# RWKV-7 chunk scan: solution and next chunk's values by turns, last chunk's output behind them; the heads of the A products and the halves of the merge by turns

## The chip, the cores and the metric

The kernel runs on one NeuronCore of one Trainium2 chip. A core has a matrix engine (PE, with its weight loads listed as PEld), a vector engine (DVE), a scalar engine (ACT), a general engine (POOL) and a queue engine (SP), each with its own in-order instruction stream, and 16 DMA engines. The metric is the device time in microseconds; lower is better. [...]

## The reference

One decoder block, sequence 2048, width 1024, float32. One projection of the normed input feeds two token mixers; their outputs are projected, gated, merged, projected again and added to the residual stream. The change lies in the second mixer, a delta-rule recurrence with 16 heads of width 64:

```
def step(state, inp):
    r_t, w_t, k_t, v_t, kk_t, b_t = inp
    sk = jnp.einsum('bhvk,bhk->bhv', state, kk_t)
    state = (state * w_t[:, :, None, :] - sk[..., None] * b_t[:, :, None, :]
             + v_t[..., None] * k_t[:, :, None, :])
    return state, jnp.einsum('bhvk,bhk->bhv', state, r_t)
```

## The kernel before

The sequence is cut into 4 blocks of 512 tokens (`b`), the heads into 4 groups of 4 (`g`), so there are 16 calls of `group`. A group holds two pairs of heads (`q`), a pair two heads (`hh`), and a block 8 chunks of 64 tokens (`c`, with `e = c % 2`). Inside a chunk the recurrence is solved in closed form:

- `pair` prepares one pair of heads. It projects keys, receptances and values (`shifted`, whose products are recorded at L195 in the helper `mm3k`), forms `KR` and `BK`, and multiplies them into the score matrices ("A products", L525), which DVE masks into `As` (L527). The stationary operand there is `BKz`, a copy of `BK` in which the other head's 64 rows are zero, so that each product uses all 128 rows. ACT makes that copy (L518).
- `group` then inverts the triangular 64x64 blocks in `As`: the 32x32 diagonal blocks on POOL (L594 and L596), and the off-diagonal 32x32 blocks by two rounds of products ("the merge", L626 and L635), first all of `e = 0`, then all of `e = 1`, in one PSUM bank `pq`.
- The chunk scan runs over the 8 chunks. PE multiplies the state into `xo` (L668) and adds the part that comes from the chunk's own values `uv` (L673). DVE copies that to `X` (L676). PE multiplies `X` by the inverse (the solution, L682), DVE scales it into `uv` (L684), PE forms the state's update (L688), and DVE applies it (L693). The chunk's output `o` (`olast`, L653) is formed one chunk later and copied by ACT (L655).

A PE product uses as many rows of the array as its operands have partitions, and as many columns as its output has. A product on fewer than 128 rows or columns stands on a tile of the array; which one follows from the start partitions of operands (rows) and output (columns). `prow(e)` and `vrow(e)` name the two halves of the partitions, swapped between even and odd chunks. In before the scan uses 64x64 tiles (L673, L682), 128x64 tiles (L653) and the whole array (L668, L688); the profile writes this as `64*64`, `128*64`, `128*128`. A float32 product is two PE instructions (hence L525 x1024 for 512 products). The projections are float32r, one instruction each.

The order on each engine is made by a list scheduler from the program order and priorities before the kernel runs. While a scan waits, it puts projections (L195) of the gates and the convolution in between. Scan, A products and merge of one group therefore lie among the projections and preparation of others.

Of the kernel before, what the change touches and what calls it, by code (L numbers as in the profile page):

```python
# [2 lines left out]

# [6 lines left out]
F32 = mybir.dt.float32  # L10
# [3 lines left out]
ALU = mybir.AluOpType  # L14
# [4 lines left out]
P = 128  # L19
# [4 lines left out]
CH = 64  # L24
NCH = TB // CH
# [57 lines left out]
def hybrid_block(ctx: ExitStack, tc: tile.TileContext, x, vecs, convk, w2a2, final_g, ada, w_in, w_co, w_ro, w_o, crow, out,  # L83
                 seq=2048, groups=(0, 1, 2, 3), phase2=True, dbg=None):
    nc = tc.nc
# [46 lines left out]
    def flat(ap):  # L132
        return ap.rearrange("p a b -> p (a b)")
# [114 lines left out]
    pa = late.enter_context(tc.tile_pool(name="pa", bufs=PAB, space=PSUM))  # L248
# [23 lines left out]
    def headsum(ps, full, hi):  # L272
# [4 lines left out]
    BKz = c1.tile([P, 2, NCH // 2, 4 * CH], F32, name="BKz")  # L277
    nc.gpsimd.memset(BKz[64:128, 0], 0.0)
    nc.gpsimd.memset(BKz[0:64, 1], 0.0)
    hones = bones.bitcast(F32)[:, 0::64]  # L280
    one = c1.tile([P, CH], F32, name="one")
    nc.vector.memset(one, 1.0)
    maskA = c1.tile([P, 4, CH], F32, name="maskA")
# [154 lines left out]
    def prow(e):  # L438
        return slice(64, 128) if e == 0 else slice(0, 64)

    def vrow(e):
        return slice(0, 64) if e == 0 else slice(64, 128)

    kcol, rcol = prow, vrow

    def pair(b, q_, pr, h, lora, uv, Asb, rn, res):
# [12 lines left out]
        pq = pa.tile([P, TB], F32, name="aux", tag="aux")  # L459
# [12 lines left out]
        pe = l3.tile([P, NCH], F32, name="pe", tag="pe", bufs=4)  # L472
# [3 lines left out]
        KR = l3.tile([P, NCH // 2, 4 * CH], F32, name="KR", tag="KR", bufs=KRB)  # L476
        BK = l3.tile([P, NCH // 2, 4 * CH], F32, name="BK", tag="BK", bufs=BKB)
# [14 lines left out]
        for c in range(NCH):  # L492
            nc.tensor.matmul(pss[prow(c % 2), c // 2, :], sq[:, c * CH:c * CH + CH], hones, start=True, stop=True,
                             skip_group_check=True)
# [6 lines left out]
                                       scalar=hkk[:, pr:pr + 1], in1=E2.rearrange("p (c n) -> p c n", n=2 * CH),  # L501
                                       op0=ALU.mult, op1=ALU.mult)
# [13 lines left out]
        for hh in range(2):  # L516
            hs = slice(64 * hh, 64 * hh + 64)
            nc.scalar.copy(BKz[hs, hh], BK[hs])  # L518
        for c4 in range(NCH // 4):
            for hh in range(2):  # L520
                pA = pa.tile([P, 2, 256], F32, name="aux", tag="aux")
                for c in range(4):
                    cc, e = (c4 * 4 + c) // 2, c % 2
                    es = slice(e * 128, e * 128 + 128)
                    nc.tensor.matmul(pA[:, c // 2, es], BKz[:, hh, cc, es], KR[:, cc, es],  # L525
                                     start=(c == 0), stop=(c == 3), skip_group_check=True)
                nc.vector.tensor_tensor(  # L527
                    out=Asb[:, hh, c4 * 4:c4 * 4 + 4, :].rearrange("p (a e) n -> p a (e n)", e=2),
                    in0=pA, in1=flat(maskA).unsqueeze(1).broadcast_to([P, 2, 256]), op=ALU.mult)
        for e in range(2):  # L530
            sl = prow(e)
            tri = Asb[sl, :, e::2, kcol(e)]
# [18 lines left out]
        tk = l3.tile([P, NCH, P], F32, name="tk", tag="tk", bufs=TKB)  # L551
# [8 lines left out]

    def group(b, g, h, lora, fill):
        uv = l3.tile([P, NCH, 2, P], F32, name="uv", tag="uv", bufs=2)
        As = [l3.tile([P, 2, NCH, P], F32, name="As", tag="As", bufs=ASB) for _ in range(2)]
        R = [{}, {}]
        rn = lt.tile([P, 2, NCH // 2, 2], F32, name="rn", tag="rn")
# [51 lines left out]
        pq = pl.tile([P, 2, 2, NCH // 2, 32], F32, name="late", tag="late")  # L617
        for e in range(2):
            lo_, hi_ = quarters(e)
            for q in range(2):  # L620
                for hh in range(2):
                    nc.vector.transpose(T11[lo_, q, hh], As[q][lo_, hh, e::2, lo_])
        for e in range(2):
            lo_, hi_ = quarters(e)
            for n, (q, hh, c) in enumerate(every):
                nc.tensor.matmul(pq[hi_, q, hh, c, :], As[q][lo_, hh, 2 * c + e, hi_], T11[lo_, q, hh, c, :],  # L626
                                 start=(n == 0), stop=(n == 15), skip_group_check=True)
        for e in range(2):
            lo_, hi_ = quarters(e)
            nc.vector.tensor_copy(Qs[hi_], pq[hi_])  # L630

        for e in range(2):
            lo_, hi_ = quarters(e)
            for n, (q, hh, c) in enumerate(every):
                nc.tensor.matmul(pq[lo_, q, hh, c, :], Qs[hi_, q, hh, c, :], As[q][hi_, hh, 2 * c + e, hi_],  # L635
                                 start=(n == 0), stop=(n == 15), skip_group_check=True)
        for e in range(2):
            lo_, hi_ = quarters(e)
            for q in range(2):
                nc.vector.tensor_copy(As[q][lo_, :, e::2, hi_], pq[lo_, q])  # L640


        O = uv[:, 0::2]
        Sg = S[g]
        prev = None

        def olast(c, xo):

            vr, rc = vrow(c % 2), rcol(c % 2)
            for q in range(2):  # L650
                for hh in range(2):
                    hs = slice(64 * hh, 64 * hh + 64)
                    nc.tensor.matmul(xo[vr, q, hs], As[q][:, hh, c, rc], uv[:, c, q, hs],  # L653
                                     start=False, stop=(q == 1 and hh == 1), skip_group_check=True)
            nc.scalar.copy(O[vr, c // 2], xo[vr, 0:2])  # L655

        for c in range(NCH):
            cc, e = c // 2, c % 2
            pr_, vr = prow(e), vrow(e)
# [6 lines left out]
            xo = px.tile([P, 4, P], F32, name="xo", tag="xo")  # L666
            for q in range(2):
                nc.tensor.matmul(xo[:, q, :], R[q]["KR"][:, cc, es], Sg[:, q, :], start=(q == 0), stop=False,  # L668
                                 skip_group_check=True)
            for q in range(2):  # L670
                for hh in range(2):
                    hs = slice(64 * hh, 64 * hh + 64)
                    nc.tensor.matmul(xo[pr_, q, hs], As[q][vr, hh, c, kcol(e)], uv[vr, c, q, hs],  # L673
                                     start=False, stop=False, skip_group_check=True)
            X = lt.tile([P, 2, P], F32, name="X", tag="X", bufs=1)
            nc.vector.tensor_copy(X[pr_], xo[pr_, 0:2])  # L676
            if prev:
                olast(*prev)
            for q in range(2):
                for hh in range(2):  # L680
                    hs = slice(64 * hh, 64 * hh + 64)
                    nc.tensor.matmul(xo[pr_, q, hs], As[q][pr_, hh, c, kcol(e)], X[pr_, q, hs],  # L682
                                     start=(q == 0 and hh == 0), stop=(q == 1 and hh == 1), skip_group_check=True)
            nc.vector.tensor_tensor(out=uv[pr_, c].rearrange("p q (h n) -> p q h n", n=64),  # L684
                                    in0=xo[pr_, 0:2].rearrange("p q (h n) -> p q h n", n=64),
                                    in1=rn[pr_, :, cc, :].unsqueeze(3).broadcast_to([64, 2, 2, 64]), op=ALU.mult)
            for q in range(2):
                nc.tensor.matmul(xo[:, 2 + q, :], R[q]["tk"][:, c, :], uv[:, c, q, :], start=False, stop=(q == 1),  # L688
                                 skip_group_check=True)
            for q in range(2):  # L690
                for hh in range(2):
                    hs = slice(64 * hh, 64 * hh + 64)
                    nc.vector.scalar_tensor_tensor(out=Sg[hs, q, hs], in0=xo[hs, 2 + q, hs],  # L693
                                                   scalar=R[q]["pe"][hs, c:c + 1], in1=Se[hs, q, hs],
                                                   op0=ALU.mult, op1=ALU.add)
            prev = (c, xo)
        olast(*prev)


        O16 = O.rearrange("p a q (h n) -> p a (q h) n", n=64)  # L700
# [426 lines left out]
```

## Time and profile before

| | before |
|---|---|
| median of 3 runs | 3123.53 us (3115.43 to 3130.16) |
| profiled execution | 3119.74 us |
| its span | 3118.0 us |
| PE busy | 2980.5 us (96%) |
| DVE busy | 2138.2 us (69%) |
| POOL busy | 1142.4 us (37%) |
| ACT busy | 1018.6 us (33%) |
| mean granted TensorE clock | 0.984 |

Busy time on PE counts an instruction from its start to a modelled end, and instructions overlap there, so the rate at which PE works is read from the distance between starts, in the timeline of instructions. In that view a row is a run of like instructions of a line: start, time to the end of the last, number. The 16 groups lie between about 90 and 2640 us of the span; behind them come the output projections.

### The profile page before, as it was taken

What the parts mean: (1) busy time and instruction counts of PE and PEld (TensorE: products, weight loads), DVE (VectorE), ACT (ScalarE), POOL (GpSimd) and SP (SyncE); (2) the same over time, 40 slices, a digit from 0 to 9 for tenths busy, and PEclk for the clock granted to TensorE, in tenths of its full rate; (3) what the DMA queues carried; (4) which work ended last, traced back from release to release, by engine and by line L of the source; (5) the groups of instructions that cost most, each with busy time, mean ns of one, the idle gap of its engine ahead of it and who ended that gap; (6) DMA issues with size and microseconds to landing.
All of it is one profiled execution on the core that took longest, in us unless ns stands there. A gap on an engine that the chain in (4) does not pass through costs nothing. (4 is left out here: it accounts for less than half of the span.)

```text
span 3118.0 us, 64926 instructions
## 1 busy us (share of the span) xinstructions
PE 2980.5 (96%) x25648; PEld 2804.4 (90%) x25648; DVE 2138.2 (69%) x4282; ACT 1018.6 (33%) x1868; POOL 1142.4 (37%) x1708
## 2 busy tenths in 40 slices
PE   6799998999999999999999999999999999799998
PEld 6689998989999999999999999999999978678888
DVE  6676867686767676767676677767688535986633
ACT  4424343433233332323232414132332213342311
POOL 3354435433433325142424335316256013653100
PEclk9899999999999999999999999999999999899999
DMA  7665758573747476547565767646458657777665
GB/s 297 214 239 193 258 187 278 192 236 133 251 139 256 136 242 230 197 138 233 159 221 166 260 211 262 196 142 208 139 178 267 215 204 271 282 250 274 216 223 176
DMA packets 354849, 667.79 MB, mean 214 GB/s; under 512 B 134704, under 2 KB 153456, under 8 KB 354544
## 3 DMA queue, kind: packets, MB, share of 16 engines
q1 hardware_dynamic: 354544, 663.64, 63.2%
q8 instruction: 202, 3.31, 0.4%
q14 instruction: 103, 0.84, 0.1%
HBM read 483.07 MB, written 179.31 MB: 212 GB/s over the span
## 5 line engine op out<-in xcount | busy, mean ns | idle before, releaser
L195 PE MATMUL ps_main<-h_hi,w_hi 128*128 128x256 f32 x4608 | 958.1, 285 | 24.4 <-ACT w_hi L178 19.1
L195 PE MATMUL ps_main<-h_hi,w_lo 128*128 128x256 f32 x4608 | 958.6, 285 | 9.0 <-POOL w_lo L180 7.6
L195 PE MATMUL ps_main<-h_lo,w_hi 128*128 128x256 f32 x4608 | 958.1, 285 | 0.0
L195 PEld LDWEIGHTS ps_main<-h_hi,w_hi 128*128 128x128 f32 x4608 | 718.3, 189 | 35.9 <-ACT w_hi L178 20.2
L195 PEld LDWEIGHTS ps_main<-h_hi,w_lo 128*128 128x128 f32 x4608 | 716.7, 189 | 18.0 <-POOL w_lo L180 9.4
L195 PEld LDWEIGHTS ps_main<-h_lo,w_hi 128*128 128x128 f32 x4608 | 716.3, 189 | 7.3 <-issue 0.7
L759 DVE SCALAR_TENSOR_TENSOR acc<-u,ck,acc 128x512 f32<-128x512 f32 x928 | 698.0, 752 | 20.1
L594 POOL TENSOR_TENSOR itmp<-La,TT 128x126 f32<-128x126 f32 (+22 forms) x496 | 179.4, 362 | 147.5 <-DMA La<-dA 112.0
L693 DVE SCALAR_TENSOR_TENSOR S<-xo,pe,Se 64x64 f32<-64x64 f32 x512 | 144.9, 283 | 107.9 <-PE xo L688 98.6
L178 ACT CAST w_hi<-w_st 128x1024 fp32r<-128x1024 f32 x103 | 107.9, 1048 | 293.7 <-DMA w_st<-w_in_t 144.0
L596 POOL TENSOR_TENSOR TT<-TT,itmp 128x126 f32<-128x126 f32 (+22 forms) x496 | 190.0, 383 | 35.8
L663 ACT ACTIVATE Se<-S,pe 128x128 f32<-128x128 f32 x256 | 88.9, 394 | 228.7 <-DVE S L693 228.3
L180 POOL TENSOR_TENSOR w_lo<-w_st,w_hi 128x1024 fp32r<-128x1024 f32 x47 | 112.2, 2388 | 136.8 <-ACT w_hi L178 98.2
L548 POOL TENSOR_TENSOR vv<-rk,vv 128x512 f32<-128x512 f32 x32 | 43.5, 1359 | 295.7 <-ACT rk L547 295.7
L684 DVE TENSOR_TENSOR uv<-xo,rn 64x256 f32<-64x256 f32 x128 | 53.8, 421 | 131.8 <-PE xo L682 130.7
L525 PE MATMUL aux<-KR,BKz 128*128 128x128 f32 x1024 | 136.6, 278 | 2.6 <-DVE As L527 1.8
L180 DVE TENSOR_TENSOR w_lo<-w_st,w_hi 128x1024 fp32r<-128x1024 f32 x56 | 75.6, 1349 | 82.4 <-PE ps_main L195 51.3
L525 PEld LDWEIGHTS aux<-KR,BKz 128*128 128x128 f32 x1024 | 123.8, 191 | 5.0 <-DVE As L527 2.0
L527 DVE TENSOR_TENSOR As<-aux,maskA 128x512 f32<-128x512 f32 x128 | 86.9, 687 | 46.7 <-PE aux L525 46.1
L676 DVE COPY X<-xo 64x256 f32<-64x256 f32 x128 | 53.7, 420 | 91.6 <-PE xo L673 90.7
L655 ACT COPY uv<-xo 64x256 f32<-64x256 f32 x128 | 46.8, 366 | 186.2 <-PE xo L653 185.7
L668 PE MATMUL xo<-S,KR 128*128 128x128 f32 x512 | 95.7, 279 | 1.2 <-DVE S L693 1.1
(290 smaller groups left out, 5497.5 us busy)
## 6 DMA issues: line engine op xcount, KB each, us to landing
w_hi<-kh_in SPq DMA_DIRECT2D x219, 512.0 KB, 3.9
w_lo<-kl_in SPq DMA_DIRECT2D x219, 512.0 KB, 5.0
w_st<-w_in_t SPq DMA_DIRECT2D x73, 512.0 KB, 4.6
kh_in<-w_hi SPq DMA_DIRECT2D x71, 512.0 KB, 3.0
kl_in<-w_lo SPq DMA_DIRECT2D x71, 512.0 KB, 4.5
w_hi<-kh_ro SPq DMA_DIRECT2D x32, 512.0 KB, 4.3
w_lo<-kl_ro SPq DMA_DIRECT2D x32, 512.0 KB, 5.8
w_st<-w_co_t SPq DMA_DIRECT2D x32, 512.0 KB, 3.5
```

The costliest lines, as they stand in the source:

```text
L178: nc.scalar.copy(hi, st)
L180: lo_eng.tensor_tensor(out=lo, in0=st, in1=hi.bitcast(F32), op=ALU.subtract)
L195: nc.tensor.matmul(ps[:, qs], ww[:, k, :], aa[k][:, qs], start=(k == 0 and t == 0 and q == 0), stop=(k == KT - 1 and t == 2 and q == ms - ...
L525: nc.tensor.matmul(pA[:, c // 2, es], BKz[:, hh, cc, es], KR[:, cc, es], start=(c == 0), stop=(c == 3), skip_group_check=True)
L527: nc.vector.tensor_tensor(out=Asb[:, hh, c4 * 4:c4 * 4 + 4, :].rearrange("p (a e) n -> p a (e n)", e=2), in0=pA, in1=flat(maskA).unsqueeze ...
L594: nc.gpsimd.tensor_tensor(out=tmp[:, :ni, :nt], in0=La[:, j:j + 1, j + 1:].broadcast_to([P, ni, nt]), in1=TT[:, :ni, j:j + 1].broadcast_to ...
L596: nc.gpsimd.tensor_tensor(out=TT[:, :ni, j + 1:], in0=TT[:, :ni, j + 1:], in1=tmp[:, :ni, :nt], op=ALU.add)
L663: nc.scalar.mul(Se[:, q, :], Sg[:, q, :], R[q]["pe"][:, c:c + 1])
L668: nc.tensor.matmul(xo[:, q, :], R[q]["KR"][:, cc, es], Sg[:, q, :], start=(q == 0), stop=False, skip_group_check=True)
L684: nc.vector.tensor_tensor(out=uv[pr_, c].rearrange("p q (h n) -> p q h n", n=64), in0=xo[pr_, 0:2].rearrange("p q (h n) -> p q h n", n=64) ...
L693: nc.vector.scalar_tensor_tensor(out=Sg[hs, q, hs], in0=xo[hs, 2 + q, hs], scalar=R[q]["pe"][hs, c:c + 1], in1=Se[hs, q, hs], op0=ALU.mult ...
L759: nc.vector.scalar_tensor_tensor(out=acc if i + 1 < HALO else yj, in0=u[:, i:i + TB], scalar=ck[:, j, i:i + 1], in1=acc, op0=ALU.mult, op1 ...
```

## The change

Three places are changed.

**A products.** `BKz` and its copies go. Each head's product takes its own 64 rows of `BK` and `KR` (a 64x128 tile), and the program writes the two heads by turns, into two PSUM buffers `pA[0]` and `pA[1]` that are both taken before the first product.

**Merge.** The two halves `e` get a PSUM bank each (`pq[1]` from the pool `aux`, which `pair` uses as well), and the products of the halves are written by turns, in a fixed order (`issue_after` keeps an instruction behind another on its engine).

**Scan.** The solution and the values' part are products on 128 rows: `Xz` and `uv` hold zeros in the other 64 rows (POOL clears `uv` at each group's start, L563, and `Xz` once). The values' part of chunk `c + 1` (`xval`) is written by turns with the solution of chunk `c`, and `olast(c - 1)` follows directly; ACT copies the values' part to `Xz` (`xcopy`), and DVE adds the state's part to it in place of the copy to `X`. The two PSUM tiles `xo` belong to even and odd chunks throughout a group.

```
         for c4 in range(NCH // 4):
+            pA = [pa.tile([P, 2, 256], F32, name="aux", tag="aux") for _ in range(2)]
...
+                for hh in range(2):
+                    hs = slice(64 * hh, 64 * hh + 64)
+                    nc.tensor.matmul(pA[hh][:, c // 2, es], BK[hs, cc, es], KR[hs, cc, es],
+                                     start=(c == 0), stop=(c == 3), skip_group_check=True)
             for hh in range(2):
-                pA = pa.tile([P, 2, 256], F32, name="aux", tag="aux")
...
-                    nc.tensor.matmul(pA[:, c // 2, es], BKz[:, hh, cc, es], KR[:, cc, es],
...
+        for e in range(2):
+            nc.gpsimd.memset(uv[prow(e), e::2], 0.0)
...
+        pq = [p_.tile([P, 2, 2, NCH // 2, 32], F32, name=n_, tag=n_) for p_, n_ in ((pl, "late"), (pa, "aux"))]
...
+            for n, (q, hh, c) in enumerate(every[::-1]):
+                for e in range(2):
+                    with tc.issue_after(mm[-1].ins) if mm else nullcontext():
+                        mm_ = mul(e, q, hh, c, dict(start=(n == 0), stop=(n == 15), skip_group_check=True))
+                    mm = mm if n else mm + [mm_]
...
+        xo = [px.tile([P, 4, P], F32, name="xo", tag="xo") for _ in range(2)]
...
+            nc.tensor.matmul(xo[c % 2][prow(c % 2), 2 + q, hs], As[q][:, hh, c, kcol(c % 2)], uv[:, c, q, hs],
+                             start=(n == 0), stop=(n == 3), skip_group_check=True)
...
+            nc.scalar.copy(Xz[prow(c % 2), c % 2], xo[c % 2][prow(c % 2), 2:4])
...
-                    nc.tensor.matmul(xo[pr_, q, hs], As[q][vr, hh, c, kcol(e)], uv[vr, c, q, hs],
...
-            nc.vector.tensor_copy(X[pr_], xo[pr_, 0:2])
-            if prev:
-                olast(*prev)
...
-                    nc.tensor.matmul(xo[pr_, q, hs], As[q][pr_, hh, c, kcol(e)], X[pr_, q, hs],
...
+            nc.vector.tensor_tensor(out=Xz[pr_, e], in0=b_[pr_, 0:2], in1=Xz[pr_, e], op=ALU.add)
...
+            for n, (q, hh, hs) in enumerate(every):
+                with tc.issue_after(mm.ins) if n else nullcontext():
+                    mm_ = nc.tensor.matmul(b_[pr_, q, hs], As[q][:, hh, c, kcol(e)], Xz[:, e, q, hs],
+                                           start=(n == 0), stop=(n == 3), skip_group_check=True)
+                mm = mm if n else mm_
+                if c + 1 < NCH:
+                    with tc.issue_after(mm.ins):
+                        xval(c + 1, n)
+            if c:
+                with tc.issue_after(mm.ins):
+                    olast(c - 1)
+            if c + 1 < NCH:
+                xcopy(c + 1)
+            if c:
+                ocopy(c - 1)
```

Lines of the changed kernel that the prediction names: A products L523, merge L636 and L640, values' part L664, its copy L668, `olast` L673, its copy L677, state products L690, solution L697, state update L714.

PE in the middle of the program, one chunk of a scan in before (L668 state, L673 values, L653 last chunk's output, L682 solution, L525 A products of the next group's pair, L195 projections; an x count is in products):

```order
L668 MATMUL xo<-S_427,KR 128x128
L673 MATMUL xo<-uv,As 64x64 x4
L653 MATMUL xo<-uv,As 64x64 x4
L195 MATMUL ps_main<-h_lo,w_hi 128x256 x2
L195 MATMUL ps_main<-h_hi,w_lo 128x256 x2
L195 MATMUL ps_main<-h_hi,w_hi 128x256 x2
L195 MATMUL ps_main<-h_lo,w_hi 128x256 x2
L525 MATMUL aux<-KR,BKz 128x128 x4
L195 MATMUL ps_main<-h_hi,w_lo 128x256 x2
L195 MATMUL ps_main<-h_hi,w_hi 128x256 x2
L525 MATMUL aux<-KR,BKz 128x128
L682 MATMUL xo<-X,As 64x64 x4
```

PE in the changed kernel, likewise one chunk in the middle of the program (L697 solution, L664 next chunk's values, L673 last chunk's output):

```order
L195 MATMUL ps_main<-h_hi,w_lo 128x256 x2
L697 MATMUL xo<-Xz,As 64x64
L664 MATMUL xo<-uv,As 64x64
L697 MATMUL xo<-Xz,As 64x64
L664 MATMUL xo<-uv,As 64x64
L697 MATMUL xo<-Xz,As 64x64
L664 MATMUL xo<-uv,As 64x64
L697 MATMUL xo<-Xz,As 64x64
L664 MATMUL xo<-uv,As 64x64
L673 MATMUL xo<-uv,As 64x64 x4
L195 MATMUL ps_main<-h_hi,w_hi 128x256 x2
```

Two runs of small products became one run, by turns; it holds in every chunk but the last of a group, whose solution has no next chunk beside it.

PE in the changed kernel, A products of two pairs; the buffer number behind `aux` tells the two heads apart:

```order
L673 MATMUL xo_5475<-uv_4664,As_4668 64x64 x2
L523 MATMUL aux_7049<-KR_6893,BK_6894 128x128
L523 MATMUL aux_7050<-KR_6893,BK_6894 128x128
L523 MATMUL aux_7049<-KR_6893,BK_6894 128x128
L523 MATMUL aux_7050<-KR_6893,BK_6894 128x128
L523 MATMUL aux_7049<-KR_6893,BK_6894 128x128
L523 MATMUL aux_7050<-KR_6893,BK_6894 128x128
L523 MATMUL aux_7049<-KR_6893,BK_6894 128x128
L523 MATMUL aux_7050<-KR_6893,BK_6894 128x128
```

```order
L195 MATMUL ps_main_24112<-h_hi_23628,w_hi_24108 128x256 x2
L523 MATMUL aux_23990<-KR_23815,BK_23816 128x128 x4
L714 MATMUL xo_22607<-uv_21832,tk_22146 128x128
L714 MATMUL xo_22607<-uv_21832,tk_22405 128x128
L523 MATMUL aux_23991<-KR_23815,BK_23816 128x128 x4
```

The first piece stands by turns, as the program is written. In the second the scheduler had one buffer before the other, and each head's four products stand by themselves.

More of the change, by code (lines that the diff above doesn't have):

```diff
@@ L616, in group @@
         every = [(q, hh, c) for q in range(2) for hh in range(2) for c in range(NCH // 2)]
-        pq = pl.tile([P, 2, 2, NCH // 2, 32], F32, name="late", tag="late")
-        for e in range(2):
+        pq = [p_.tile([P, 2, 2, NCH // 2, 32], F32, name=n_, tag=n_) for p_, n_ in ((pl, "late"), (pa, "aux"))]
+        for e in (1, 0):
             lo_, hi_ = quarters(e)
@@ L663, in group @@
                 nc.scalar.mul(Se[:, q, :], Sg[:, q, :], R[q]["pe"][:, c:c + 1])
-            xo = px.tile([P, 4, P], F32, name="xo", tag="xo")
             for q in range(2):
-                nc.tensor.matmul(xo[:, q, :], R[q]["KR"][:, cc, es], Sg[:, q, :], start=(q == 0), stop=False,
+                nc.tensor.matmul(b_[:, q, :], R[q]["KR"][:, cc, es], Sg[:, q, :], start=(q == 0), stop=False,
                                  skip_group_check=True)
[L670 to L674, printed above, removed]
@@ new lines, in group @@
+            for n, (q, hh, hs) in enumerate(every):
+                with tc.issue_after(mm.ins) if n else nullcontext():
[8 more added lines that the diff above has]
+                    olast(c - 1)
@@ L687, in group @@
             for q in range(2):
-                nc.tensor.matmul(xo[:, 2 + q, :], R[q]["tk"][:, c, :], uv[:, c, q, :], start=False, stop=(q == 1),
+                nc.tensor.matmul(b_[:, 2 + q, :], R[q]["tk"][:, c, :], uv[:, c, q, :], start=False, stop=(q == 1),
                                  skip_group_check=True)
[L690 to L695, printed above, removed]
@@ L696, in group @@
-            prev = (c, xo)
-        olast(*prev)
+            for q, hh, hs in every:
+                nc.vector.scalar_tensor_tensor(out=Sg[hs, q, hs], in0=b_[hs, 2 + q, hs],
+                                               scalar=R[q]["pe"][hs, c:c + 1], in1=Se[hs, q, hs],
+                                               op0=ALU.mult, op1=ALU.add)
+        olast(NCH - 1)
+        ocopy(NCH - 1)
         O16 = O.rearrange("p a q (h n) -> p a (q h) n", n=64)
```

70 lines of the change are left out of this document (32 added, 38 removed).

## The prediction

> **What bounds the kernel now.** First the page's engine rows, then the stretch that holds the scans (group 0's preparation lies ahead of it), and what PE waits for there.
>
> ```profile
> span 3118.0 us, 64926 instructions
> PE 2980.5 (96%) x25648; PEld 2804.4 (90%) x25648; DVE 2138.2 (69%) x4282; ACT 1018.6 (33%) x1868; POOL 1142.4 (37%) x1708
> 230.00:2640.00 2410.00, 2370.81 (x21822) 2262.90 (x21820) 1673.72 (x3408) 792.66 (x1460) 909.32 (x1490) 1.00 0.62 206
> PE ps_main L195 <- ACT w_hi L178: 9.9, 3, 6.8
> PE xo L682 <- DVE X L676: 2.9, 4, 1.2
> PE xo L688 <- DVE uv L684: 1.9, 3, 1.0
> PE xo L668 <- DVE S L693: 1.1, 2, 0.6
> ```
>
> The third row gives, for 230 to 2640 us, PE, PEld, DVE, ACT and POOL busy time, then the granted clock. PE is busy for 2370.8 of 2410 us at full clock; DVE for 69%. The last four rows are PE's waits in that stretch: the three links of the scan's chain cost it 5.9 us in nine waits over fifteen groups, because projections stand in between. So PE's own instruction stream is the bound, and I count what the change does to that stream.
>
> Busy time on PE overlaps, so rates come from starts in the timeline (start, us, instructions, count).
>
> ```profile
> 1382.71 0.38 PE L668 MATMUL xo<-S,KR 128*128 128x128 f32 x2
> 1383.02 0.67 PE L673 MATMUL xo<-uv,As 64*64 64x64 f32 x8
> 1383.63 0.68 PE L653 MATMUL xo<-uv,As 128*64 128x64 f32 x8
> 1384.23 0.39 PE L195 MATMUL ps_main<-h_lo,w_hi 128*128 128x256 f32 x1
> 1384.46 0.40 PE L195 MATMUL ps_main<-h_hi,w_lo 128*128 128x256 f32 x2
> 1384.69 0.40 PE L195 MATMUL ps_main<-h_hi,w_hi 128*128 128x256 f32 x2
> 547.36 0.44 PE L682 MATMUL xo<-X,As 64*64 64x64 f32 x4
> 547.73 0.38 PE L195 MATMUL ps_main<-h_hi,w_lo 128*128 128x256 f32 x1
> 902.39 1.95 PE L525 MATMUL aux<-KR,BKz 128*128 128x128 f32 x16
> 904.10 0.36 PE L195 MATMUL ps_main<-h_hi,w_lo 128*128 128x256 f32 x1
> ```
>
> A projection instruction takes 0.118 us (two in 0.23). An A-product instruction takes 0.107 us (16 in 1.71). Eight small ones with the change of tile behind them take 0.60 us (1383.63 to 1384.23), four take 0.37, so one takes 0.058. From 1382.71 to 1384.46 lie 1.75 us; two L668, sixteen small ones and one L195 make 0.21 + 0.93 + 0.12 = 1.26. The other 0.49 us belong to three changes of tile size: 0.16 us each.
>
> **The change part by part.** Its main question is whether products on different tiles run side by side. Three places of before, where neighbours happen to lie on different tiles, speak to it.
>
> ```profile
> 853.71 0.68 PE L682 MATMUL xo<-X,As 64*64 64x64 f32 x8
> 854.32 0.63 PE L493 MATMUL aux<-bones,sq 128*64 128x2 f32 x16
> 854.88 0.50 PE L195 MATMUL ps_main<-h_lo,w_hi 128*128 128x256 f32 x2
> 886.86 0.62 PE L653 MATMUL xo<-uv,As 128*64 128x64 f32 x7
> 887.26 0.22 PE L493 MATMUL aux<-bones,sq 128*64 128x2 f32 x1
> 887.32 0.22 PE L653 MATMUL xo<-uv,As 128*64 128x64 f32 x1
> 977.50:977.75 0.25, 0.25 (x14) 0.25 (x11) 1.00 1.04 311
> 978.00:978.12 0.12, 0.12 (x14) 0.12 (x10) 1.00 1.33 393
> L626 PE MATMUL late<-T,As 32*32 32x32 f32 x1024 | 36.0, 193 | 0.8 <-DVE T L622 0.5 <-ACT xTs L345 0.2
> ```
>
> L493 alternates between the two column halves: its sixteen instructions take 0.56 us with the change behind them, where eight on one half take 0.61. At 887.26 an L493 instruction starts before the last L653 ahead of it: the tile, not the queue, is what it waits for. The two stretch rows hold L626 alone: 14 instructions touch the 0.25 us inside one half `e`, and 14 touch 0.125 us across the border from one half to the other. An instruction lasts 0.193 us, so some six of each 14 had started earlier; eight starts take 0.25 us on one tile (0.031 each) and 0.125 us (0.016) where two tiles meet. I take two tiles by turns at half the price.
>
> *Scan.* Per chunk the same twelve small products remain; on 128 rows instead of 64 they cost the same (L673 and L653 above, 0.61 and 0.60 us for eight). In 7 of 8 chunks the four solutions and four next values stand by turns in the changed order: 16 x 7 x 4 = 448 pairs. A pair saves two instructions of 0.058 us, less some 0.01 us of stagger: 448 x 0.105 = **47 us**.
>
> [...]
>
> *Merge.* 502 of 512 pairs stand by turns. A pair is four instructions, 0.124 us one after the other and 0.064 by turns: 502 x 0.06 = **30 us**.
>
> *A products.* 512 products, two instructions of 0.107 each. By turns as written they would save half. In the changed order most don't stand so: of 116 runs only 16 are eight by turns, 24 are four of one head alone; counting neighbours of different heads once each gives 129 pairs. 129 x 2 x 0.107 = **27 us**. No row of before shows two tiles that differ in rows alone; the bounds are 0 and 27, and I take 27, since L626 overlaps where rows and columns differ.
>
> *Changes of tile size.* In the orders I count 821 in before and 645 in the changed kernel. The scan's and merge's fall to 413; the A products, now on 64 rows, bring 232 that were not there (38 us, more than their turns save). Net 176 x 0.16 = **28 us**. What the new 64x128 size costs to enter is not shown: between 0 and 0.16 each, so up to 38 us better.
>
> *Beside PE.*
>
> ```profile
> L655 ACT COPY uv<-xo 64x256 f32<-64x256 f32 x128 | 46.8, 366 | 186.2 <-PE xo L653 185.7
> L518 ACT COPY BKz<-BK 64x1024 f32<-64x1024 f32 x64 | 66.9, 1046 | 35.2 <-POOL BK L506 29.9 <-DVE BK L500 4.3 <-DVE ss L335 0.2
> L676 DVE COPY X<-xo 64x256 f32<-64x256 f32 x128 | 53.7, 420 | 91.6 <-PE xo L673 90.7
> L684 DVE TENSOR_TENSOR uv<-xo,rn 64x256 f32<-64x256 f32 x128 | 53.8, 421 | 131.8 <-PE xo L682 130.7
> L278 POOL MEMSET BKz<- x1: 950/950/950, 1.1 to 1.1; 64x1024 f32 x1
> 1556.30 1.90 POOL L719 TENSOR_TENSOR uv<-uv,grs 128x1024 f32<-128x1024 f32 x1
> 1564.74 0.60 PE L724 MATMUL late<-ident,uv 128*128 128x128 f32 x4
> ```
>
> ACT gains 128 copies of 0.366 (47 us) and loses 67; it is at 33%. DVE's copy becomes an addition at the price of L684, the same 0.42 us. POOL gains 32 clears of `uv` at 0.95 (30 us of its 1500 idle). A clear needs the buffer that the transposes of L724 read last, so POOL stands from the end of L719 to theirs: 7 us here (1558.2 to 1565.3), with the next convolution's halo copy and weight splits queued behind it; in the order that copy serves a convolution one later, so I charge nothing, at most 15 x 7 = 105 us of POOL.
>
> Both `aux` buffers of `pA` are now taken together, so the next eight products wait for two masks.
>
> ```profile
> L527 DVE TENSOR_TENSOR As<-aux,maskA 128x512 f32<-128x512 f32 x128 | 86.9, 687 | 46.7 <-PE aux L525 46.1
> L525 PE MATMUL aux<-KR,BKz 128*128 128x128 f32 x1024 | 136.6, 278 | 2.6 <-DVE As L527 1.8 <-ACT BKz L518 0.8
> ```
>
> That is 2 x 0.69 us, 64 times: from 0 to 88 us. PE stands 1.8 us for it in before, since projections fill in; I take it into the waits below.
>
> *Sum.* 47 + 30 + 27 + 28 = 132 us off PE's stream. Given back: 3 us, since group 0's A products and merge lie where PE stands anyway, and 11 us for new waits, as DVE's share of a shorter stretch rises to 1674 / 2280 = 73% (PE's three chain waits, 5.9 us now, would have to triple). Net 118: 3119.7 - 118 = **3002 us**. The sum stands on the profiled execution, 3.8 us under the median of 3123.5. Its own range is 2960 to 3045: 38 less if the new size is free, 27 + 16 more if the A heads don't overlap and waits double.
>
> **The rivals.**
>
> *Column halves don't overlap while both stream 64 columns.* Then the scan's 47 us stay: 3049. For it: L493 moves 2 columns only. Against: L653 streams 64 columns beside L493, and its last instruction starts 0.06 us behind the L493 (887.26, 887.32), its usual pace. [...]
>
> *No turns overlap at all*, the change doesn't do what it says: only the 28 us of changes come, less about 4 of waits: 3096. The L626 border speaks against it.
>
> *More than the sum:* the 64x128 size is entered free and no wait comes: 3119.7 - 129 - 38 = 2953.
>
> *Slower: the scan's ring through ACT.* In the changed order DVE's addition (and with it every convolution tap behind it on DVE) waits for ACT's copy of the values, and L690 waits for the bank that ACT's output copy releases. ACT is in order, and a weight cast or a copy for another pair can stand first.
>
> ```profile
> L178 ACT CAST w_hi<-w_st 128x1024 fp32r<-128x1024 f32 x103 | 107.9, 1048 | 293.7 <-DMA w_st<-w_in_t 144.0 <-DMA w_st<-w_co_t 63.4 <-issue 46.7
> ```
>
> If every chunk is late by half a cast, 0.52, and both copies, 0.73, PE loses 128 x 1.25 = 160 us: 3162. It decides from 118 / 128 = 0.92 us a chunk, where the gain is used up. Against it: in the changed order the median is 25 projection instructions, 3.0 us, between a run of small products and L714, and as many again up to L690, so ACT has some 6 us.
>
> **How the numbers follow.** Forecast 0.67; column halves 0.11 (3049); nothing overlaps 0.07 (3096); more 0.07 (2953); slower 0.08 (3162). The range from 2950 to 3095 takes in the first, second and fourth and leaves out the slower case and some of the third. What a measurement can tell from no change is 0.5%, 15.6 us, so faster means under 3104: 0.67 + 0.11 + 0.07 + 0.02 of the third = 0.87; same 0.05; slower 0.08.
>
> **What would show it.** L697 and L664 in the timeline: eight products (16 instructions) and the four L673 behind them in about 1.1 us from first start to the next L195; if about 1.5, column halves don't overlap. L636 and L640: 64 instructions in about 1.1 us where L626 took 2.0. An L523 run of eight by turns in about 1.1 us against 1.8; a run of four alone in 0.9 plus 0.3 for the two changes. PE's waits on DVE's `Xz` and on ACT small, a few us. The forecast is wrong if L697 waits for `Xz` by over 1 us a chunk, or if the span of the scans (230 to 2640) does not shrink by over 100 us.

## The result, and the profile after

The change moved nothing: a median of 3120.4 us (20 runs, 3110.9 to 3131.1) against 3120.5 for before in the same comparison (20 runs), ratio 0.9998 with an interval of 0.9988 to 1.0008. The forecast was 3002 and the range ended at 3095: the result lies above it. The profiled execution took 3120.46 us.

The engine rows, and the row of the scans' stretch (PE, PEld, DVE, ACT, POOL, clock, DMA share, GB/s), of after:

```profile
span 3118.7 us, 65148 instructions
PE 2902.9 (93%) x25648; PEld 2724.8 (87%) x25648; DVE 2152.8 (69%) x4282; ACT 998.4 (32%) x1932; POOL 1170.4 (38%) x1739
230.00:2640.00 2410.00, 2297.66 (x21801) 2183.83 (x21801) 1717.28 (x3432) 780.17 (x1532) 955.61 (x1527) 0.96 0.62 206
```

PE's share fell from 96% to 93%, and in the stretch of the scans the granted clock from 1.00 to 0.96. What PE waits for there (us in total, times, longest):

```profile
PE xo L714 <- DVE uv L710: 18.3, 11, 5.2
PE xo L664 <- DVE As L651: 13.6, 5, 6.2
PE xo L697 <- DVE Xz L692: 12.3, 9, 3.8
PE ps_main L195 <- ACT w_hi L178: 7.3, 3, 3.7
PE xo L690 <- DVE S L717: 3.8, 3, 1.8
PE xo L690 <- ACT Xz L668: 1.6, 3, 0.7
```

The three chain waits (on `Xz`, `uv` and `S`) were 5.9 us in before and are 34.4 now, in few and long pieces. One stretch of after, then the same microseconds in before:

```profile
1150.00:1178.00 28.00, 18.09 (x205) 14.90 (x206) 20.51 (x39) 10.75 (x22) 15.75 (x17) 0.51 0.41 132
```

```profile
1150.00:1178.00 28.00, 28.00 (x347) 26.70 (x346) 16.46 (x40) 12.21 (x23) 13.12 (x14) 1.00 0.67 213
```

PE is busy for 18 of 28 us in after, with a granted clock of 0.51; in before it is busy for all 28, at 1.00. So PE's time has three parts, and I split both traces that way. From each product's start to the next start is *work*; where the next start lies over 0.05 us behind the end of everything that runs, that piece is *idle*. Where the clock is halved, half of the time from start to start counts as work and the other half as *half clock*. Some 30 us of each span lie before the first product and behind the last. In us, for all kernels of this study whose runs were timed:

| kernel | median | ratio, interval | work | idle | half clock |
|---|---|---|---|---|---|
| before | 3120 to 3125 | 1 | 2943.7 | 107.8 | 36.6 |
| after | 3120.4 | 0.9998 (0.9988, 1.0008) | 2811.8 | 188.1 | 90.9 |
| e1 scan alone | 3135.8 | 1.0046 (1.0028, 1.0063) | 2842.0 | 191.7 | 70.4 |
| e2 merge alone | 3181.8 | 1.0186 (1.0172, 1.0200) | 2916.1 | 150.3 | 81.2 |
| e3 A products alone | 3163.0 | 1.0121 (1.0105, 1.0136) | 2948.3 | 115.3 | 70.6 |
| e4 scan and merge | 3120.0 | 0.9985 (0.9973, 0.9996) | 2813.8 | 193.4 | 78.2 |
| e5 after, solution and values twice | 3191.9 | 1.0221 (1.0197, 1.0245) | 2873.9 | 190.0 | 97.5 |
| e6 before, solution twice | 3190.5 | 1.0221 (1.0191, 1.0251) | 3001.1 | 107.0 | 50.5 |
| e7 after, one weight buffer more | 3089.1 | 0.9881 (0.9862, 0.9901) | 2809.1 | 171.5 | 82.0 |
| e8 after, retuned | 3074.5 | 0.9839 (0.9819, 0.9859) | 2815.1 | 158.7 | 74.2 |
| e10 after, A products tied by turns | 3098.0 | 0.9930 (0.9913, 0.9947) | 2817.9 | 177.8 | 70.5 |
| e11 after, prefix sums behind | 3115.9 | 0.9974 (0.9960, 0.9987) | 2814.4 | 174.9 | 102.4 |
| e12 e10 and retuned | 3046.9 | 0.9763 (0.9749, 0.9778) | 2812.5 | 151.3 | 53.9 |
| e13 before, merge in two banks | 3179.5 | 1.0177 (1.0141, 1.0212) | 2954.6 | 135.5 | 58.2 |
| e14 A products alone, tied | 3143.9 | 1.0058 (1.0034, 1.0082) | 2939.0 | 120.5 | 54.8 |
| e15 merge by turns, one bank | 3153.1 | 1.0094 (1.0062, 1.0125) | 2913.5 | 143.2 | 62.5 |

From before to after, work falls by 131.9 us, idle rises by 80.3 and half clock by 54.3: the whole saving came, and 134.6 us went back.

### The profile page after: what moved, and what is told of

The parts are those of the page before. It is cut to its first block, busy times and chain, and to the rows that moved or that the text cites. A ratio compares the mean times of both kernels' runs of the same rounds, so it can differ in the third digit from the quotient of the medians.

```text
span 3118.7 us, 65148 instructions
## 1 busy us (share of the span) xinstructions
PE 2902.9 (93%) x25648; PEld 2724.8 (87%) x25648; DVE 2152.8 (69%) x4282; ACT 998.4 (32%) x1932; POOL 1170.4 (38%) x1739
## 4 chain that ended last, share of the span: by engine, by line
PE 52%; DVE 15%; DMA 15%; POOL 8%; issue 4%; SPq 3%; ACT 3%; POOLq 0%; DVEq 0%; ACTq 0%
PE ps_main L195 37%; DMA w_st<-w_in_t 3%; PE aux L523 3%; POOL TT L597 3%; POOL itmp L595 3%; DVE acc L783 2%; DVE M L466 2%; SPq L608 2%; DMA La<-dA 1%; PE xo L697 1%; DMA dT<-TT 1%; PE pout L1072 1%; PE pout L1073 1%; PE xo L714 1%; PE pout L1071 1%
## 5 line engine op out<-in xcount | busy, mean ns | idle before, releaser
L195 PE MATMUL ps_main<-h_hi,w_hi 128*128 128x256 f32 x4608 | 961.0, 287 | 31.6 <-ACT w_hi L178 20.9
L195 PE MATMUL ps_main<-h_hi,w_lo 128*128 128x256 f32 x4608 | 964.0, 287 | 12.8 <-POOL w_lo L180 8.4
L195 PE MATMUL ps_main<-h_lo,w_hi 128*128 128x256 f32 x4608 | 965.0, 287 | 0.0
L195 PEld LDWEIGHTS ps_main<-h_hi,w_hi 128*128 128x128 f32 x4608 | 724.3, 192 | 42.3 <-ACT w_hi L178 22.2
L195 PEld LDWEIGHTS ps_main<-h_hi,w_lo 128*128 128x128 f32 x4608 | 724.3, 191 | 25.1 <-POOL w_lo L180 10.7
L195 PEld LDWEIGHTS ps_main<-h_lo,w_hi 128*128 128x128 f32 x4608 | 725.1, 192 | 8.2 <-issue 0.5
L783 DVE SCALAR_TENSOR_TENSOR acc<-u,ck,acc 128x512 f32<-128x512 f32 x928 | 698.1, 752 | 21.8
L180 POOL TENSOR_TENSOR w_lo<-w_st,w_hi 128x1024 fp32r<-128x1024 f32 x47 | 113.0, 2404 | 113.6 <-ACT w_hi L178 100.5
L668 ACT COPY Xz<-xo 64x256 f32<-64x256 f32 x128 | 46.8, 365 | 263.2 <-PE xo L673 229.5
L523 PE MATMUL aux<-KR,BK 64*128 64x128 f32 x1024 | 126.1, 308 | 4.4 <-DVE As L526 3.5
L710 DVE TENSOR_TENSOR uv<-xo,rn 64x256 f32<-64x256 f32 x128 | 53.8, 420 | 100.5 <-PE xo L697 90.3
L523 PEld LDWEIGHTS aux<-KR,BK 64*128 64x128 f32 x1024 | 102.5, 203 | 20.2 <-DVE As L526 3.6
L526 DVE TENSOR_TENSOR As<-aux,maskA 128x512 f32<-128x512 f32 x128 | 84.1, 687 | 42.4 <-PE aux L523 41.7
L690 PE MATMUL xo<-S,KR 128*128 128x128 f32 x512 | 101.0, 291 | 5.6 <-DVE S L717 3.8
L692 DVE TENSOR_TENSOR Xz<-xo,Xz 64x256 f32<-64x256 f32 x128 | 53.7, 420 | 75.3 <-PE xo L690 70.4
```

The lines of the kernel that those rows point to most:

```text
L180: lo_eng.tensor_tensor(out=lo, in0=st, in1=hi.bitcast(F32), op=ALU.subtract)
L195: nc.tensor.matmul(ps[:, qs], ww[:, k, :], aa[k][:, qs], start=(k == 0 and t == 0 and q == 0), stop=(k == KT - 1 and t == 2 and q == ms - ...
L523: nc.tensor.matmul(pA[hh][:, c // 2, es], BK[hs, cc, es], KR[hs, cc, es], start=(c == 0), stop=(c == 3), skip_group_check=True)
L526: nc.vector.tensor_tensor(out=Asb[:, hh, c4 * 4:c4 * 4 + 4, :].rearrange("p (a e) n -> p a (e n)", e=2), in0=pA[hh], in1=flat(maskA).unsqu ...
L690: nc.tensor.matmul(b_[:, q, :], R[q]["KR"][:, cc, es], Sg[:, q, :], start=(q == 0), stop=False, skip_group_check=True)
L783: nc.vector.scalar_tensor_tensor(out=acc if i + 1 < HALO else yj, in0=u[:, i:i + TB], scalar=ck[:, j, i:i + 1], in1=acc, op0=ALU.mult, op1 ...
```

## The experiments

**The parts by themselves (e1 to e4).** e1 is the scan of after in before, with two start-up tiles moved into another tile's space and the constant `one` cut to one column, to make room beside `BKz`; e2 is the merge of after in before; e3 its A products; e4 is after with before's A products and the same room made. Their edits are the parts of the diff above.

> The scan's change alone; A products and merge as before. (To make room for Xz beside BKz, two start-up tiles share another tile's space and the constant `one` is read from one column.) Theory A, waits come from how the merge and the A products stand in the order (few projections between their steps): PE's small products shrink by some 85 to 95 us as in the changed kernel, waits stay near before's 32 us in the scans, time 3030 to 3060. Theory B, the scan's ring through ACT and the addition on DVE causes the waits: PE waits on Xz, uv and S grow by 30 us and the half clock behind them by as much, 3090 to 3120. Theory C, something else than PE sets about 3118 whatever PE does: 3110 to 3125, with the waits as large as the saving.

> The merge's change alone. Theory A: the merge's products shrink by 24 us, but waits at the groups' starts (As, merge, first chunk) and the half clock behind them give back 30 to 60: 3125 to 3155. Theory B: only the 24 us come: 3093 to 3100. Theory C: 3115 to 3125, waits up by 24.

> The A products' change alone. All theories agree on PE's own price: changes of tile size eat what the turns save (112 us before, 118 in the changed kernel): 3115 to 3130. Theory A adds waits for the two aux buffers, up to 20 us: 3120 to 3145.

> Scan and merge changed, A products as before (same room-making edits as the scan alone). PE's small products shrink by about 115 us. Theory A, with the merge as the cause: waits of 60 us and the half clock, 3090 to 3125, clearly above the scan alone. Theory A, with the A products as the cause: 3000 to 3030. Theory B: 3085 to 3110. Theory C: 3110 to 3125.

Each part alone is slower than before, by 0.5, 1.9 and 1.2%, and scan and merge together stand where after stands. So it is not one bad part that eats the gain of the others. e1's work is 102 us less than before's, and 84 us of idle and 34 of half clock cancel it. e2's work is 28 less for 43 and 45 more. e3 saves nothing in work and loses 34 us to the clock, with hardly more idle (7.5 us). A stretch of it without any idle time; in its first row PE works on 64 merge instructions (32 rows) and 16 instructions of the A products (64 rows) at full clock, and the half clock lies in the second, 0.67 over 10.20 us:

```profile
1175.40:1178.80 3.40, 3.40 (x80) 3.36 (x78) 1.38 (x2) 0.62 (x1) 2.76 (x4) 1.00 0.70 210
1178.80:1189.00 10.20, 10.20 (x106) 9.76 (x105) 5.80 (x12) 2.46 (x4) 2.54 (x2) 0.67 0.66 190
```

The parts don't add: 11.6, 57.6 and 38.8 us by the medians, and together nothing. The scheduler makes a new order for each kernel, and each order has its own waits. Each part alone came out above every range set for it, so no theory had its price. A rival stays open: e3 loses 39 us, and e13 below 55, with no work taken off PE, so part of every loss here may be that a new order is not fitted to the tables and buffers as before's is.

**Does PE's work still set the time? (e5, e6)** If something off PE had become the bound, more work on PE would be free in after and dear in before.

```
-            for n, (q, hh, hs) in enumerate(every):
+            for n, (q, hh, hs) in list(enumerate(every)) * 2:
```

> The changed kernel with the burst of solution and values issued twice in every chunk (the second pass overwrites the first with the same numbers): 128 times 8 or 16 more small instructions, 0.46 us each time, 59 us of PE work. Theory W (PE still carries the time, the waits lie between its work): 3160 to 3190. Theory F (something else, off PE, is the floor at about 3118): 3115 to 3135, the added work goes into the waits.

> The kernel before with the solution's products issued twice in every chunk, 128 x 8 instructions of 0.058 us = 59 us of PE work. Both theories: 3170 to 3195, since PE is the bound in before; if it rises by less than 40, the twin run of the changed kernel can't tell the theories apart.

e6 is the same edit on the solution in before. e5 does 62 us more work than after and takes 71 us longer; e6 does 57 more than before and takes 66 longer. Added work is paid in full, in both, and e5's idle stays at 190. So no other engine's own work sets a floor at 3120. The added products lie in the scan's chain, though, so these runs don't tell whether PE's stream or that chain sets the time. Idle and half clock lie at places where PE has nothing to do, and this work doesn't fill them.

**Buffers for weights (e7) and a new order (e8).** The projections are PE's cover, and they wait for weights (L195 on `w_hi`: 7.3 us in three waits in after). e7 gives the weights' pool a seventh buffer in the room that `BKz` left.

```
-WB = 6
+WB = 7
```

> The changed kernel with one weight buffer more (WB = 7), in the memory that BKz left. If the waits come from weights and splits that arrive late (L195 waits on w_hi, w_lo and the stored copies), PE's idle time falls by 15 to 30 us and the half clock with it: 3075 to 3105. If they come from the scan's chain on DVE and ACT alone: 3110 to 3130.

e8 also changes the table of what projections go ahead in which group, and gives ACT one of the two copies between the merge's rounds, that of the half `e = 0`; after has both on DVE.

```
-LP = "cgcg cgcg cc ccgg gg"
+LP = "cggc cgcg ccg ccg gg"
...
-            nc.vector.tensor_copy(Qs[hi_], pq[e][hi_])
+            (nc.vector.tensor_copy if e else nc.scalar.copy)(Qs[hi_], pq[e][hi_])
```

> The changed kernel with one weight buffer more, another order of the last block's projections (LP) and the first of the two copies behind the merge on ACT instead of DVE. Theory W: the forecast saving on PE is there and only the cover was lost, so with cover rearranged idle and half clock fall from 279 to about 210 us: 3045 to 3080. Theory F: 3110 to 3130 whatever the order.

One buffer is worth 31 us against after, the rest 15 more, at the same work; idle falls by 17 and 13, half clock by 9 and 8. In before that room is taken: such a buffer is 4 KB a partition, and e1 had to make room beside `BKz` for the 2 KB of `Xz`. So the memory that the change freed is what pays here; a seventh buffer in before was not run. Before with another table, or with that copy on ACT, was not run, so how much of the 15 us, and of e12 below, it could have had too stays open.

**A products held by turns (e10).** In after the scheduler tears most heads apart. Here each product is tied behind the other head's.

```
+                    with tc.issue_after(mA.ins) if mA else nullcontext():
+                        mA = nc.tensor.matmul(pA[hh][:, c // 2, es], BK[hs, cc, es], KR[hs, cc, es],
```

> The changed kernel with the A products tied in their written order, so that each eight stand by turns on PE. PE's time for them falls from 105 us to 75 to 85 at full clock. If the waits stay as they are: 3090 to 3105. If eight products that wait for two buffers together cost new waits: 3110 to 3130.

22 us faster than after, but not for the reason given: the A products' work falls only from 105 to 97 us. Half clock falls by 20 (90.9 to 70.5) and idle by 10 (188.1 to 177.8). Two heads by turns stand on both halves of the 128 rows, four products of one head on one of them; the last section counts rows against the clock.

**Prefix sums out of the chain's way (e11).** In after PE's long chain waits have DVE late by work for a later pair. The timeline, PE and then DVE (start, us, what it waited for in brackets):

```profile
1760.88 0.22 PE L664 MATMUL xo<-uv,As 128*64 128x64 f32 x1
1766.32 1.22 PE L714 MATMUL xo<-uv,tk 128*128 128x128 f32 x4 [5.22 <-DVE uv L710]
```

```profile
1762.75 3.05 DVE L466 TENSOR_TENSOR_SCAN M<-one,M 128x64 f32<-128x64 f32 x5 [2.40 <-ACT M L458]
1765.84 0.43 DVE L710 TENSOR_TENSOR uv<-xo,rn 64x256 f32<-64x256 f32 x1
```

The solution ends near 1761.1. Ahead of the scaling L710 stand five prefix sums of the next pair; the first waits 2.40 us for ACT's decay values, and together they hold DVE until 1765.8. PE waits 5.22 us for an operation of 0.43. e11 ties a pair's eight prefix sums behind one chunk's state update, all eight behind the same.

```
+            with tc.issue_after(steps[(0, 2)[q_] + c // 8].ins) if steps else nullcontext():
                 nc.vector.tensor_tensor_scan(...)
```

> The changed kernel with the eight prefix sums of M (L466, 0.26 to 1.3 us each on DVE), which stand ahead of uv or Xz in most of PE's chain waits, tied behind the state update of a chunk of the scan that runs then: pair 0's behind chunk 0, pair 1's behind chunk 2. If DVE's order is what makes the chain late, PE's waits for uv, Xz and S fall from 34 us to under 15, with half clock: 3080 to 3105. If others take their place: 3110 to 3140.

4.5 us by the medians: a miss. (The profile is of the slowest of its ten runs, 3121.3 us.) The waits in 230 to 2640 us of e11:

```profile
PE xo L701 <- DVE Xz L696: 24.4, 13, 3.7
PE xo L718 <- DVE uv L714: 13.3, 12, 2.4
PE xo L694 <- DVE S L721: 9.3, 9, 2.3
```

47 us where after has 34. But the edit moved the prefix sums more than it took them out of the way: the eight now stand together behind the update and ahead of the next chunk's `Xz`, and PE waits 2.81 us for that one. DVE in e11:

```profile
572.06 2.83 DVE L469 TENSOR_TENSOR_SCAN M<-one,M 128x64 f32<-128x64 f32 x8
574.92 0.42 DVE L696 TENSOR_TENSOR Xz<-xo,Xz 64x256 f32<-64x256 f32 x1
```

In after prefix sums are among the three operations ahead of the late one in 21.8 of the 34.4 us (11.9 on `uv`, 9.9 on `Xz`); in e11 in none of the waits on `uv` and in 13.8 us on `Xz`, and the waits behind other operations have grown from 12.6 to 33 us. That DVE's queue delays the chain is seen in both traces; how much the prefix sums cost by themselves this run doesn't tell.

**All of it (e12).** WB 7, e8's copy, e10's ties and a third table `"cgcg cgcg ccg ccg gg"`.

> All that helped, together: one weight buffer more, LP by another order, the first copy behind the merge on ACT, A products tied by turns. If PE's saved work now comes through: 3040 to 3070, faster than before by 1.7 to 2.7%. If the retuned version above (3074.5) is already at what the waits allow: 3070 to 3085.

3046.9 us, 2.4% under both kernels, at after's work: idle is 37 less and half clock 37 less than in after. It still has 44 and 17 more than before, with PE at 94%:

```profile
PE 2866.4 (94%) x25648; PEld 2682.9 (88%) x25648; DVE 2151.7 (71%) x4266; ACT 1004.9 (33%) x1948; POOL 1173.1 (39%) x1739
```

**The price of the second bank and of torn turns (e13 to e15).** e13 is before with one edit, the merge's halves in a bank each, the products in before's order. e14 is e3 with e10's ties. e15 is e2 with both halves in one bank.

```
-        pq = pl.tile([P, 2, 2, NCH // 2, 32], F32, name="late", tag="late")
+        pq = [p_.tile([P, 2, 2, NCH // 2, 32], F32, name=n_, tag=n_) for p_, n_ in ((pl, "late"), (pa, "aux"))]
```

> The kernel before with a PSUM bank for each half of the merge, the second from the pool aux, as in the changed kernel, but the products half after half in their old order: no change in PE's work. If the second bank, taken from the A products' two, is what costs the merge alone its 60 us: 3145 to 3180. If the turns and their fixed order do: 3118 to 3130.

> The A products' change alone, tied so that each eight stand by turns. If the loss of the A products alone (3163) lies in the torn turns, four of one head on 64 rows with two changes of tile: 3115 to 3130, with less half clock (71 us there). If it lies in taking both buffers together: 3145 to 3165.

> The merge's change alone, by turns as in the changed kernel, but with both halves in one PSUM bank, as before. If the second bank is the cause: 3095 to 3115, the 28 us of work come through in part. If the turns' fixed order is the cause, with no projection between the products and the copies: 3150 to 3185. It also shows whether turns overlap within one bank.

The edit that takes the second bank costs 55 us by itself (e13), nearly all of e2's 58. By turns in one bank (e15) 28 remain, though work is 30 less than before's. That lies in the range set for the turns' fixed order as the cause, where e13 lies in the range set for the bank: beside the turns the bank makes about half of the merge's loss, and what makes the other half, the fixed order or less work on PE, is not told apart. Nor is it in e13 whether the bank is missed or only the order is new. The A products alone lose 39 us torn (e3) and 19 tied (e14), the latter between the ranges of both causes that were named for it. PE's waits in 230 to 2640 us of e13, on the merge's and on the chain's row:

```profile
PE aux L626 <- DVE T L622: 9.4, 8, 2.7
PE xo L668 <- DVE S L693: 5.5, 7, 1.5
```

**Tiles by themselves (e9).** Six stretches of small products at the start of before, each behind 64 products on the whole array: 64x64 on one tile, on two column halves by turns, 128x64, 64x128 on one tile, on two row halves by turns, 32x32 on two tiles by turns. It adds these products and leaves nothing out; its single run of 3259.1 us is not compared.

> The kernel before with stretches of one kind of small product put ahead of its work, back to back and without a wait, each 13 to 15 us long at full clock, 64 products on the whole array between them: 64x64 on one tile, 64x64 by turns on two column halves, 128x64 on one tile, 64x128 on one tile, 64x128 by turns on two row halves, 32x32 by turns on two tiles. Theory U (the clock goes by the share of the array in use: in the six kernels traced so far the 3.41 us windows with less than about 0.34 of the array in use were followed by half clock): half clock in the 64x64 stretch on one tile (share about 0.23) and in the 32x32 stretch (0.1), full clock in the four others (0.45 or more). Theory B (the clock goes by busy time): full clock in all. It also gives by-turns prices for two column halves and for two row halves: half of one tile's price if they overlap.

The stretches in that order (after the comma PE busy and its instructions; the clock is third from the end):

```profile
20.00:34.00 14.00, 14.00 (x240) 13.88 (x239) 12.08 (x29) 1.45 (x2) 4.50 (x3) 1.00 1.03 411
49.00:62.50 13.50, 13.50 (x468) 13.50 (x466) 0.00 (x0) 1.05 (x1) 0.00 (x0) 1.00 0.34 133
78.00:91.00 13.00, 13.00 (x227) 13.00 (x225) 0.00 (x0) 0.00 (x0) 0.00 (x0) 1.00 0.00 1
106.50:120.00 13.50, 13.50 (x123) 13.50 (x122) 0.00 (x0) 0.00 (x0) 0.00 (x0) 1.00 0.00 1
135.50:149.00 13.50, 13.50 (x246) 13.50 (x244) 0.00 (x0) 0.00 (x0) 0.00 (x0) 1.00 0.01 2
168.50:192.40 23.90, 22.88 (x695) 22.42 (x688) 0.00 (x0) 0.00 (x0) 0.00 (x0) 0.50 0.02 4
```

The time by the count gives 58, 29, 57, 110, 55 and 34 ns an instruction, the last at half clock. Two tiles by turns cost half of one: 29 against 58 ns on column halves, 55 against 110 on row halves. 64x64 on one tile, a quarter of the array, kept a clock of 1.00 for 14 us, where theory U had half clock. 32x32 by turns went to half clock behind a pause of 0.81 us in PE's issue and stood at 0.50 for the 23.9 us of the last row, with PE busy for 22.9 of them, where theory B had full clock. Both theories of that run fall.

## Why the prediction was wrong

**Right: the overlap.** One chunk of after in the timeline:

```profile
1385.05 0.27 PE L697 MATMUL xo<-Xz,As 128*64 128x64 f32 x1
1385.05 0.27 PE L664 MATMUL xo<-uv,As 128*64 128x64 f32 x1
...
1385.51 0.22 PE L664 MATMUL xo<-uv,As 128*64 128x64 f32 x1
1385.56 0.63 PE L673 MATMUL xo<-uv,As 128*64 128x64 f32 x8
1386.12 0.51 PE L195 MATMUL ps_main<-h_hi,w_hi 128*128 128x256 f32 x2
```

1.07 us to the next projection, where 1.1 was to show overlap and 1.5 its absence. The rivals "column halves don't overlap" and "no turns overlap at all" are refuted. These pairs stand on the same 128 rows and differ in the column half alone; e9's two column halves, on the same 64 rows, show the same for streams of 64 columns, 29 against 58 ns. The merge's 64 instructions take 1.13 us, an A run of eight by turns 1.10 (expected 1.1 each).

**Right in sum: the 132 us.** Work by class, before to after: solution, values and `olast` 234.1 to 147.7, state and update 112.2 to 100.5, merge 66.6 to 36.9, A products 111.8 to 105.1; the rest is 2.5 up. Scan and merge saved 128 where the terms (47 + 30 and 65 for their changes of tile) gave 142; the A products saved 7 where 27 - 37 was a loss of 10. That it comes to 131.9 is partly errors that cancel.

**Wrong: "Given back … 11 us for new waits".** This term measured 134, and the net of 118 came to nothing. It failed in three ways.

First, the waits were sized by DVE's share of busy time, 69% to 73%, from three chain waits of 5.9 us. Those rose to 34.4 without DVE being much busier (1674 to 1717 us in the stretch).

At the link with the largest wait, the one on `uv`, both traces show what changed. From the end of the solution PE had 3.05 us of work (median of the 128 chunks) until it needed `uv` in before, and 2.98 in after: that cover hardly changed. But `uv` came 0.79 us in mean after the solution in before, with 11 chunks over 2 us, and 1.20 us in after, with 28. Kernels with the new scan have 1.20 (e1) and 1.30 (e4), kernels with the old one 0.76 (e3) and 0.73 (e13). So DVE answers late in more chunks, which its mean share of busy time doesn't show. Prefix sums of a later pair are often ahead of it (e11), but whether the chain would be on time without them is not shown.

For the rest of the idle time one reading is that work taken off PE is cover taken away: e1, with 102 us less work, has 84 more of idle. That is argued, not shown: no run put the cover back without the work, and e13 gains 28 us of idle with no work saved. The growth of the three chain waits is 28.5 of the 80 us. From 230 us to the scans' last update idle went from 33.9 to 102.5 us, in the tail from 38 to 48.

Small waits on DVE's `Xz` and on ACT were the mark set for it; `Xz` is 12.3 us in nine waits, below the 1 us a chunk that was named, and so this mark would have missed the loss, which lay beside it on `uv` and `As`. The other mark held: the last update comes at 2564 us in place of 2596, 32 us earlier and not over 100.

Second, the sum had no term for the clock. Long waits were paid twice here, as idle time and as half clock, and e3's stretch of small tiles went to half clock without a wait (0.67 over 10.20 us). Of the 54 us that half clock added, 56 came in the scans (9.2 to 65.5) and the rest gave 2 back. In that stretch of after, half clock came with or right behind each single wait of over 2.2 us, for 3.4 to 27 us.

Third, resources that two parts share were taken at nothing. Both `aux` buffers at once were bounded at 0 to 88 us and put "into the waits below", and the merge's bank out of that pool got no price at all; e13 measures that edit at 55 us in before. The waits for the A products' own buffers stayed small: 3.5 us in after (L523 for the masks L526), 1.8 in before. The 13.6 us on `As` (L664; 1.2 in before) are something else, the first chunk of a group waiting for the merge's last copies (L651), and the sum had no term for that either.

**The slower rival** did not occur as told: PE's wait on ACT's `Xz` (L668) is 1.6 us in three. Its place was right in part, the chain of solution and values, but the late engine is DVE. "More than the sum" did not occur either.

**Open.** Which of DVE's operations delay the chain is different in each order, and e11 doesn't tell what they cost apart. Why the three parts lose 108 us apart and nothing together is not known. The part of the merge's loss that is left in e15 is not explained.

## What to carry to other kernels

PE was busy for 96% of the time here, and 132 us less work on it gave nothing, while the three chain waits grew from 5.9 to 34.4 us: what is saved on the busiest engine can be lost where the engines in its chains answer late. Their mean busy share did not tell that (DVE 69% before and after): look at how late their answers come, chunk by chunk, and against how much work in between. Check the clock as a second price of long waits; half clock grew by 54.3 us here. Ask of every part which shared bank or buffer it takes, and measure that edit by itself. A change that is right in its work may only pay once order and buffers are fitted to it: here the same work took 3120 us and then 3047, though what the same fitting would give before was not run.

## What the runs showed of the hardware

In the clock records of before and after the granted share is 1 or 0.5. Of their 47 stretches at 0.5, 45 are whole multiples of 3.41 us long, from 3.4 to 27.3 us; the other two run into the end of the program. They came behind idle time (in after a wait of 5.22 us, then 10.2 us at half clock) and without it (e3, above).

What tells such steps apart is an estimate of mine, fitted to this case's profiles. For each step of 3.41 us at full clock between 230 and 2640 us of the seventeen profiles I counted the rows of the array in use over the step. A product counts with its share of the 128 rows, for the time its columns take at the pace of the A products: 107 ns for 128 columns of float32, and taken as much for 256 of float32r, whose instruction took 118. Of the 11459 steps, 244 were followed by half clock. A line drawn at 0.38 of the rows, half clock below and full clock above, has 21 steps on the wrong side. A line at 0.34 of the whole array has 35, one at 0.38 of busy time 70.

e9's stretches lie outside this count and agree with the line by rows: 64x64 alone, rows in use 0.46 of the time and 0.23 of the array, kept 1.00 for 14 us; 32x32 by turns, 0.30 of the rows in the step with the pause, went to 0.50. The line also fits e14 against e3, where the A products' tie to both row halves came with 16 us less half clock (70.6 to 54.8) and 5 us more idle (115.3 to 120.5). It was not tested with a run made for it, and why rows should go with the clock is not shown.
